# State-space tables on VectorE, merged preparation, value normalisation on ScalarE and modulation dots spread anew in a two-layer hybrid backbone

## Chip, cores and metric

One core of one Trainium2 chip. The metric is the device time of one execution in microseconds, of which the median of several runs is given; lower is better. All inputs are float32 in device memory, and one launch computes the whole output. PE is TensorE, DVE VectorE, ACT ScalarE, POOL GpSimd, SP SyncE (the engine that issues all DMA transfers here, from one queue in order).

## The reference

Two layers run over 256 latent tokens and 256 context tokens of 1024 channels. Layer 0 has a half SwiGLU (width 2816), a mixer and another half SwiGLU; layer 1 the same with attention as the mixer, and needs only the latent tokens after it. Every sub-layer is

```
h = rms(x) * g_pre * (1 + scale) + shift            # per channel
x = x + weight * gate * rms(sublayer(h)) * g_post
shift, scale, gate = columns of silu(c) @ w_mod + b_mod   # 9 x 1024 a layer, for both c
```

The mixer of layer 0 has two groups of heads side by side:

```
p = h @ w_in                                # 768 u, 768 v, 256 for the state-space part
v: gelu, in 6 groups of 128 channels: (v - mean) * rsqrt(var + eps) * g
ya = gelu(u) * (w_s @ v + b_s)              # w_s 128 x 128 over each chunk of 128 tokens
# 16 groups of 16 inputs, 64 complex states, two directions (the second runs backwards)
lam_bar = exp(lam * dt);  b_bar = (lam_bar - 1) / lam * b
s[t] = lam_bar * s[t-1] + b_bar @ u[t];     yb = real(c @ s) + d * u, then gelu and a gate
```

## The kernel before, in words

Channels or features lie on the 128 partitions. A weight chunk of 1 MB (128 x 2048) is loaded by SP into `wraw` (2 buffers), rounded on ACT to `whi` and subtracted on DVE to `wlo` (3 buffers each; `load_upto`, L662 and L663), two chunks ahead of its use; every product is three matmuls (high by high, low by high, high by low). The order of PE and POOL is that of the program text. DVE, ACT and SP are ordered by a planner with an estimated cost for each instruction; on the chip each engine then works through its list strictly in that order. `issue_after(mark)` keeps an instruction from being placed before another one, here mostly the latest gate product of the SwiGLU (L921).

*The first SwiGLU* (`ffn` with `extra=True`) has 22 weight tiles f; tiles 0 to 2 belong to the opening, and `rest(f)` does one of the others: 48 matmuls of 512 columns. After it come 11 chunks of the out projection (`out_proj`), of which the first 8 run over all four token tiles; the last 3 are held for the end, token by token, each followed by `finish` (gate, residual, norm of the next sub-layer).

*Modulation dots.* A column block of w_mod (128 columns, transposed) is multiplied with silu(c) by one DVE instruction with accumulation for each c (L702), two for most blocks and one for the 32 that only the latent needs. One block is a job: one load into `mraw` (2 buffers) and its dots. 128 jobs are handed out in order: `mods(n)` adds n to what is due and issues as many; `mods_need` issues at once whatever a boundary still lacks: `gate_rows` wants the gate's blocks, `scale_cols` the next sub-layer's shift and scale.

*State-space preparation* (`S5Prep`). `angles` and `phasors` compute cos and sin of the step's angle and square them repeatedly on [128,16] tiles on DVE (`cmul`, `unit`), `small` the decays' powers (copied into LP and WP by `put`). `table` builds powers E of the unit phasor by doubling, 1 to 128 steps in 7 levels, for a direction and half of the 8 pairs of groups: four tables, on POOL, in a single buffer `s5E`. `table_out` stores each to device memory (L227). `pair(q)` multiplies the coefficients with B and C on DVE into zero-padded block matrices `s5bd` and `s5cz`, `pair_pe(q)` transposes and multiplies them on PE (L281, L292), `pair_out` stores the result. `s5_jobs` says after which tile f each is emitted: tables at 4, 6, 8, 10, their stores two tiles later, pairs at 12 to 19 and their PE parts one tile later. So tile f of the text is followed on PE by the transposes of pair f-13.

*The mixer* (`mixer0`): value products `value(b, w, t)` on PE for three chunks b of 256 columns and four token tiles t (24 matmuls each), gelu on ACT, mean and variance on DVE; `norm(b, t)` takes two token tiles at once: variance to DVE's copy, rstd on POOL (L751, L752), then four `tensor_scalar` on DVE (L1129). `mix(b)` is the product with w_s. Between them, `slot(k)` holds `states(k)` (PE products L355; then eight multiplications and additions and four scans on DVE, giving H) and, two slots later, `read_out(k - 2)` (PE, L389, reads H). `fill` copies the inputs u that L355 reads.

Of the kernel before, what the change touches and what calls it, by code (L numbers as in the profile page):

```python
# [40 lines left out]
class S5Prep:  # L41


    def __init__(self, K, pool, dram, small, d_bc):
# [8 lines left out]
        self.n2 = pool.tile([128, 16], I32, name="s5n2")  # L53

# [49 lines left out]
    def cmul(self, ore, oim, are, aim, bre, bim):  # L104
        V = self.K.nc.vector
        m = self.nw
        t, u = self.new(), self.new()
        V.tensor_tensor(t, are, bre, op=ALU.mult)
        V.tensor_tensor(u, aim, bim, op=ALU.mult)
        V.tensor_tensor(t, t, u, op=ALU.subtract)  # L110
        V.tensor_tensor(u, are, bim, op=ALU.mult)
        V.tensor_tensor(oim, aim, bre, op=ALU.mult)
        V.tensor_tensor(oim, oim, u, op=ALU.add)
        V.tensor_copy(ore, t)
        self.nw = m

    def unit(self, re, im):
        V = self.K.nc.vector
        m = self.nw
        t, u = self.new(), self.new()  # L120
        V.tensor_tensor(t, re, re, op=ALU.mult)
        V.tensor_tensor(u, im, im, op=ALU.mult)
        V.tensor_tensor(t, t, u, op=ALU.add)
        V.tensor_scalar(t, t, -0.5, 1.5, op0=ALU.mult, op1=ALU.add)
        V.tensor_tensor(re, re, t, op=ALU.mult)
        self.last = V.tensor_tensor(im, im, t, op=ALU.mult).ins
        self.nw = m

    def angles(self):
# [3 lines left out]
        self.dt, a, s, c = (self.new() for _ in range(4))  # L133
        self.cs = c, s
        self.exp(self.dt, ls)
        V.tensor_tensor(a, lim, self.dt, op=ALU.mult)
        self.sincos(s, c, a)

        self.ph = (self.new(), self.new())
        V.tensor_copy(self.ph[0], c)  # L140
        V.tensor_scalar(self.ph[1], s, -1.0, None, op0=ALU.mult)
        for _ in range(2):
            self.cmul(*self.ph, *self.ph, *self.ph)
            self.unit(*self.ph)

    def phasors(self):

        self.steps = [self.ph]
        for k in range(1, 7):
            br, bi = self.new(), self.new()  # L150
            self.cmul(br, bi, *self.steps[k - 1], *self.steps[k - 1])
            self.unit(br, bi)
            self.steps.append((br, bi))

    def small(self, r4):
# [4 lines left out]
        c, s = self.cs  # L160
# [7 lines left out]
        P = [(self.new(), self.new()) for _ in range(5)]  # L168
        V.memset(P[0][0], 1.0)
        V.memset(P[0][1], 0.0)  # L170
        V.tensor_tensor(P[1][0], er, c, op=ALU.mult)
        V.tensor_tensor(P[1][1], er, s, op=ALU.mult)
        for m in range(2, 5):
            self.cmul(*P[m], *P[m - 1], *P[1])

        def put(dst, src, i):
            for d in range(2):
                V.tensor_copy(dst[:, :, d, i[d]], src[:, d * 8:d * 8 + 8])

        for m in range(5):  # L180
            for ri in range(2):
                put(LP[:, ri], P[m][ri], (m, 4 - m))
        nre, den, wre, wim, t = (self.new() for _ in range(5))
        V.tensor_scalar(nre, P[1][0], -1.0, None, op0=ALU.add)
        V.tensor_tensor(den, lre, lre, op=ALU.mult)
        V.tensor_tensor(t, lim, lim, op=ALU.mult)
        V.tensor_tensor(den, den, t, op=ALU.add)
        V.reciprocal(den, den)
        V.tensor_tensor(wre, nre, lre, op=ALU.mult)
        V.tensor_tensor(t, P[1][1], lim, op=ALU.mult)  # L190
        V.tensor_tensor(wre, wre, t, op=ALU.add)
        V.tensor_tensor(wre, wre, den, op=ALU.mult)
        V.tensor_tensor(wim, P[1][1], lre, op=ALU.mult)
        V.tensor_tensor(t, nre, lim, op=ALU.mult)
        V.tensor_tensor(wim, wim, t, op=ALU.subtract)
        V.tensor_tensor(wim, wim, den, op=ALU.mult)
# [1561 lines left out]
```

## Time and profile before

| | before |
|---|---|
| time, median of 3 runs | 1644.54 us (1643.34 to 1649.43) |
| profiled execution, its own time | 1647.93 us |
| its span | 1646.2 us |
| PE busy | 1591.2 us, 97% |
| DVE busy | 1156.3 us, 70% |
| ACT busy | 645.7 us, 39% |
| POOL busy | 167.5 us, 10% |
| mean PE clock granted | 0.986 of full |

The span runs from the first to the last instruction of the profiled execution; its own time contains a little more around it. Busy shares are averages over stages that have different limits, so the stages have to be read one by one: a wait names the instruction that waited, what released it, the total, how many times and the longest. The matmuls' records overlap, so a busy PE only says that something was in the array. In the profile's names, `out<-in` is the tile written and the tiles read.

### The profile page before, as it was taken

Reading aid. Unit: us, or ns where it says so; the run is one execution under the profiler, and the core shown is the slowest. Engines: PE = TensorE matmul, PEld = TensorE weight load, DVE = VectorE, ACT = ScalarE, POOL = GpSimd, SP = SyncE. Lnnn points to the kernel's source line nnn. Section 1 sums busy time; section 2 is a strip of 40 time slices with the busy share of each in tenths; the row PEclk is TensorE's granted clock in tenths of the full one; section 3 lists DMA queues with packets and bytes.
Section 4 is the critical chain, followed back from the end, with each engine's and each line's share of the span. In section 5 each row is a group of like instructions: output and inputs, shape, how many; then the busy total and the mean of one; then the engine's idle time right before and its main releaser. Section 6 shows DMA issues by size and latency. Waiting matters only on the chain.

```text
span 1646.2 us, 23111 instructions
## 1 busy us (share of the span) xinstructions
PE 1591.2 (97%) x8916; PEld 1377.4 (84%) x8916; DVE 1156.3 (70%) x2242; ACT 645.7 (39%) x1023; POOL 167.5 (10%) x289
## 2 busy tenths in 40 slices
PE   6999779999998999999999999999999999999998
PEld 6888668888897789888888889999988877899986
DVE  6797288777689976888786367688864377576454
ACT  5422122322553454222222254466532266564343
POOL 0178600000010000000000010000000012400000
PEclk7999989999999999999999999999999999999999
DMA  9344456545335432656666222222355232146552
GB/s 366 126 160 146 153 194 194 198 171 203 138 119 180 153 125 107 226 195 218 217 225 251 100 103 77 77 103 103 124 210 179 77 119 103 65 177 248 191 192 102
DMA packets 56542, 264.04 MB, mean 160 GB/s; under 512 B 6432, under 2 KB 10992, under 8 KB 36848
## 3 DMA queue, kind: packets, MB, share of 16 engines
q1 hardware_dynamic: 56432, 262.57, 44.7%
q8 instruction: 70, 1.15, 0.3%
q14 instruction: 40, 0.33, 0.1%
HBM read 254.12 MB, written 8.43 MB: 159 GB/s over the span
## 4 chain that ended last, share of the span: by engine, by line
PE 61%; DVE 4%; issue 1%; ACT 1%; POOL 1%; POOLq 0%; DVEq 0%; ACTq 0%
PE y L823 7%; PE y L826 7%; PE y L824 7%; PE gu L816 3%; PE gu L815 3%; PE gu L817 3%; PE u L817 2%; PE g L817 2%; PE g L816 2%; PE u L816 2%; PE g L815 2%; PE u L815 2%; PE sa L534 2%; PE sa L536 2%; PE sa L535 2%
## 5 line engine op out<-in xcount | busy, mean ns | idle before, releaser
L662 ACT ACTIVATE whi<-wraw 128x2048 fp32r<-128x2048 f32 (+1 forms) x139 | 255.3, 1839 | 324.2 <-PE u L816 129.9
L663 DVE TENSOR_TENSOR wlo<-wraw,whi 128x2048 fp32r<-128x2048 f32 x131 | 300.4, 2294 | 102.1 <-ACT whi L662 101.8
L702 DVE SCALAR_TENSOR_TENSOR junkv<-mraw,cond 128x1024 bf16<-128x1024 f32 x224 | 274.6, 1226 | 89.6 <-DMA mraw<-wmod 87.3
L823 PE MATMUL y<-whi,ahi 128*128 128x512 f32 x616 | 243.7, 396 | 0.0
L824 PE MATMUL y<-wlo,ahi 128*128 128x512 f32 x616 | 243.0, 394 | 0.0
L826 PE MATMUL y<-whi,alo 128*128 128x512 f32 x616 | 198.3, 395 | 0.0
L816 PE MATMUL gu<-hlo,whi 128*128 128x256 f32 x496 | 138.7, 280 | 0.7 <-DVE hlo L807 0.7
L823 PEld LDWEIGHTS y<-whi,ahi 128*128 128x128 f32 x616 | 116.1, 188 | 27.1
L826 PEld LDWEIGHTS y<-whi,alo 128*128 128x128 f32 x616 | 116.0, 188 | 27.1
L815 PE MATMUL gu<-hhi,whi 128*128 128x256 f32 x496 | 138.6, 279 | 0.0
L824 PEld LDWEIGHTS y<-wlo,ahi 128*128 128x128 f32 x616 | 116.1, 188 | 26.8
L817 PE MATMUL gu<-hhi,wlo 128*128 128x256 f32 x496 | 138.3, 279 | 0.0
L746 POOL TENSOR_TENSOR ssy<-ssy,mh 128x1 f32<-128x1 f32 x20 | 11.8, 589 | 1220.9 <-DVE ssy L745 1220.9
L1035 ACT ACTIVATE ahi<-act 128x1024 fp32r<-128x1024 f32 (+1 forms) x44 | 41.6, 951 | 227.8 <-PE y L824 216.0
L817 PE MATMUL g<-hhi,wlo 128*128 128x512 f32 x328 | 129.3, 394 | 0.0
L817 PE MATMUL u<-hhi,wlo 128*128 128x512 f32 x328 | 129.2, 394 | 0.0
L816 PE MATMUL g<-hlo,whi 128*128 128x512 f32 x328 | 128.8, 393 | 0.0
L816 PE MATMUL u<-hlo,whi 128*128 128x512 f32 x328 | 128.6, 392 | 0.0
L815 PE MATMUL g<-hhi,whi 128*128 128x512 f32 x328 | 128.5, 392 | 0.0
L1036 DVE TENSOR_TENSOR alo<-act,ahi 128x1024 fp32r<-128x1024 f32 (+1 forms) x44 | 47.8, 1091 | 113.4 <-ACT ahi L1035 113.4
L815 PE MATMUL u<-hhi,whi 128*128 128x512 f32 x328 | 127.3, 388 | 0.0
L816 PEld LDWEIGHTS gu<-hlo,whi 128*128 128x128 f32 x496 | 93.1, 188 | 1.2 <-DVE hlo L807 1.1
(370 smaller groups left out, 3372.2 us busy)
## 6 DMA issues: line engine op xcount, KB each, us to landing
wraw<-wts SPq DMA_DIRECT2D x153, 1024.0 KB, 4.8
mraw<-wmod SPq DMA_DIRECT2D x131, 512.0 KB, 4.3
gg<-gg SPq DMA_DIRECT2D x10, 512.0 KB, 4.9
s5p<-dP SPq DMA_DIRECT2D x8, 384.0 KB, 4.9
act<-wmod SPq DMA_DIRECT2D x5, 512.0 KB, 8.7
act<-wsc SPq DMA_DIRECT2D x5, 512.0 KB, 8.5
dP<-s5cz SPq DMA_DIRECT2D x8, 320.0 KB, 2.3
dP<-s5st SPq DMA_DIRECT2D x8, 320.0 KB, 4.4
```

The costliest lines, as they stand in the source:

```text
L534: nc.tensor.matmul(o, w1[:, k], b1[:, k], start=(new and k == 0), stop=False, skip_group_check=not new)
L662: nc.scalar.activation(h, r, AF.Copy)
L663: (nc.gpsimd if pool else nc.vector).tensor_tensor(l, r, h.bitcast(F32), op=ALU.subtract)
L702: nc.vector.scalar_tensor_tensor(self.junk_v, t, 1.0, self.cond[:, s], op0=ALU.mult, op1=ALU.mult, accum_out=self.mod[:, layer, s, idx * 8 ...
L815: nc.tensor.matmul(out, w1, self.hhi[:, k, sl], start=(k == 0), stop=False)
L816: nc.tensor.matmul(out, w1, self.hlo[:, k, sl], start=False, stop=False)
L817: nc.tensor.matmul(out, w2, self.hhi[:, k, sl], start=False, stop=(k == 7))
L823: nc.tensor.matmul(o, ahi, whi[i], start=first, stop=False)
L824: nc.tensor.matmul(o, ahi, wlo[i], start=False, stop=False)
L826: nc.tensor.matmul(o, alo, whi[i], start=False, stop=last)
L1035: nc.scalar.activation(hi, src, AF.Copy)
L1036: nc.vector.tensor_tensor(lo, src, hi.bitcast(F32), op=ALU.subtract)
```

## The change

Six edits, all in layer 0 or in the handing out of the dots:

1. `table` runs on DVE; the real and the imaginary part are handled by one instruction (four instead of six a level). Tables with q0 = 0 stay in the buffer that `s5cz` shares, those with q0 = 4 lie in the buffer of the pairs' products (`s5tbc`), and two scratch tiles are shared with `s5st` and `s5bd`.
2. The complex helpers keep real and imaginary part in one [128,2,16] tile: `square` does 8 instructions where `cmul` and `unit` did 13, `cmul` 4 instead of 7; `put` is 18 ACT copies instead of 36 on DVE.
3. Tables are emitted at f = 4, 5, 6, 7, their stores one tile later, `zero` at 8, pairs at 9 to 16, their PE parts at 10 to 17.
4. Value normalisation: one small DVE instruction makes -mean x rstd, and the four big ones become ACT activations (Identity with scale and bias).
5. Dots: nothing in the opening and up to f = 5, then 1.2, 1.9 and 2.6 jobs a tile; 3 instead of 2.5 a chunk in the first out projection; the last two chunks of every out projection's main part give half; none in the mixer. `scale_cols` moves from ahead of the out projection to the first `finish`.
6. The value product of chunk 1, token tile 1, comes ahead of `slot(0)`.

```diff
-    def cmul(self, ore, oim, are, aim, bre, bim):
+    def cmul(self, o, a, b):
...
+        V.tensor_tensor(t, a, self.on2(b[:, 0]), op=ALU.mult)
+        V.tensor_tensor(u, a, self.on2(b[:, 1]), op=ALU.mult)
+        V.tensor_tensor(o[:, 0], t[:, 0], u[:, 1], op=ALU.subtract)
+        V.tensor_tensor(o[:, 1], t[:, 1], u[:, 0], op=ALU.add)
...
+    def square(self, o, a):
...
+        V.tensor_tensor(t, re, im, op=ALU.subtract)
+        V.tensor_tensor(u, re, im, op=ALU.add)
+        V.scalar_tensor_tensor(o[:, 1], re, 2.0, im, op0=ALU.mult, op1=ALU.mult)
+        V.tensor_tensor(o[:, 0], t, u, op=ALU.mult)
+        V.tensor_tensor(z, o, o, op=ALU.mult)
+        V.tensor_tensor(t, z[:, 0], z[:, 1], op=ALU.add)
         V.tensor_scalar(t, t, -0.5, 1.5, op0=ALU.mult, op1=ALU.add)
+        self.last = V.tensor_tensor(o, o, self.on2(t), op=ALU.mult).ins
...
         def put(dst, src, i):
             for d in range(2):
-                V.tensor_copy(dst[:, :, d, i[d]], src[:, d * 8:d * 8 + 8])
+                self.K.nc.scalar.activation(dst[:, :, :, d, i[d]], src[:, :, d * 8:d * 8 + 8], AF.Copy)
...
     def table(self, d, q0, pool):
+        V = self.K.nc.vector
+        if q0 == 0:
+            E = pool.tile([128, 4, 2, 128], F32, name="s5E", tag="s5big", bufs=1)
+        else:
+            E = pool.tile([128, 1152], F32, name="s5tb", tag="s5tbc", bufs=1)[:, 0:1024]
...
         for k in range(7):
             n = 1 << k
...
+            V.tensor_tensor(t, E[:, :, :, 0:n], b_r, op=ALU.mult)
+            V.tensor_tensor(u, E[:, :, :, 0:n], b_i, op=ALU.mult)
+            V.tensor_tensor(E[:, :, 0, n:2 * n], t[:, :, 0], u[:, :, 1], op=ALU.subtract)
+            V.tensor_tensor(E[:, :, 1, n:2 * n], t[:, :, 1], u[:, :, 0], op=ALU.add)
...
                 if c:
-                    self.mods(self.mod_rate)
+                    self.mods(self.mod_rate if c < n0 - 2 else self.mod_rate / 2)
...
         gg = self.gate_rows(layer, j, weight, streams)
-        if nxt:
-            self.scale_cols(*nxt)
+        todo = [nxt] if nxt else []
         def finish(t, y):
+            if todo:
+                self.scale_cols(*todo.pop())
...
-                if not extra or f < NF - 2:
+                if extra:
+                    self.mods(0 if f < 6 else 1.2 if f < 10 else 1.9 if f < 18 else 2.6)
+                else:
                     self.mods(self.mod_rate)
...
-                self.mod_rate = 2.5 if extra else 1.75
+                self.mod_rate = 3 if extra else 1.75
...
-            at(4 + 2 * i, pr.table, d, q0, pool)
-            at(6 + 2 * i, pr.table_out, d, q0)
-        at(11, pr.zero, pool)
+            at(4 + i, pr.table, d, q0, pool)
+            at(5 + i, pr.table_out, d, q0)
+        at(8, pr.zero, pool)
         for q in range(8):
-            at(12 + q, pr.pair, q, pool)
-            at(13 + q, pr.pair_pe, q, pool)
-            at(13 + q, pr.pair_out, q)
+            at(9 + q, pr.pair, q, pool)
+            at(10 + q, pr.pair_pe, q, pool)
+            at(10 + q, pr.pair_out, q)
...
                 self.rstd(r, 4)
+                nb = rs[:, 8 + 2 * t - 2:8 + 2 * t + 2]
+                V.scalar_tensor_tensor(nb.rearrange("p (t g) -> p t g", g=2), mv[:, t - 1:t + 1, :, 0], -1.0,
+                                       r.rearrange("p (t g) -> p t g", g=2), op0=ALU.mult, op1=ALU.mult)
                 for i in (t - 1, t):
                     for g in range(2):
                         v = vh[:, i, g * 128:(g + 1) * 128]
-                        V.tensor_scalar(v, v, mv[:, i, g, 0:1], rs[:, 2 * i + g:2 * i + g + 1],
-                                        op0=ALU.subtract, op1=ALU.mult)
+                        k = 2 * i + g
+                        nc.scalar.activation(v, v, AF.Identity, scale=rs[:, k:k + 1], bias=rs[:, 8 + k:9 + k])
...
-                if g >= 4:
-                    self.mods(2)
...
+            value(1, w2, 1)
             for h in hu.values():
                 self.let(h)
             slot(0)
...
-        with self.tc.issue_after(prep.last):
-            self.mods(3 * self.mod_rate)
```

## Rows read from the trace of the kernel before

**Rows 1.** The page, busy time, share of the span and instructions of each engine.

```profile
PE 1591.2 (97%) x8916; PEld 1377.4 (84%) x8916; DVE 1156.3 (70%) x2242; ACT 645.7 (39%) x1023; POOL 167.5 (10%) x289
```

**Rows 2.** Waits of PE, whole span: total us, times, longest us.

```profile
PE wbt L281 <- DVE s5bd L267: 18.1, 1, 18.1
PE s5yp L389 <- DVE s5H L376: 6.2, 3, 3.0
PE s5x L355 <- ACT u L339: 2.0, 1, 2.0
```

**Rows 3.** Windows: stretch and length, busy time (instructions) by engine, PE clock, DMA share, GB/s.

```profile
98.50:142.40 43.90, 43.90 (x194) 36.01 (x193) 42.95 (x153) 9.81 (x8) 34.66 (x46) 1.00 0.48 163
164.30:197.40 33.10, 33.10 (x145) 26.86 (x143) 8.67 (x13) 4.80 (x4) 26.17 (x58) 1.00 0.30 113
197.40:215.50 18.10, 0.03 (x1) 0.00 (x0) 10.69 (x29) 4.31 (x3) 0.95 (x1) 0.65 0.73 253
215.50:220.00 4.50, 4.46 (x24) 3.45 (x25) 4.47 (x10) 1.67 (x5) 0.00 (x0) 0.53 0.40 114
225.00:300.00 75.00, 75.00 (x406) 61.13 (x405) 60.64 (x191) 23.54 (x42) 0.00 (x0) 1.00 0.58 186
476.20:528.00 51.80, 45.53 (x321) 42.73 (x320) 47.27 (x134) 18.70 (x39) 6.92 (x10) 0.96 0.40 130
```

**Rows 4.** Waits of the DMA queue on SyncE, 40 to 300 us.

```profile
SPq L227 <- POOL s5E L224: 60.4, 3, 23.2
```

**Rows 5.** Timeline of SyncE's queue: start, duration, instruction (fourth store of a table).

```profile
196.35 0.38 SPq L227 DMA_DIRECT2D dE<-s5E  x1
```

**Rows 6.** Timeline of DVE, with the idle time before the instruction.

```profile
204.79 1.23 DVE L702 SCALAR_TENSOR_TENSOR junkv<-mraw,cond 128x1024 bf16<-128x1024 f32 x1 [17.46 <-DMA mraw<-wmod]
```

**Rows 7.** Timeline of DVE at the POOL row of the next group.

```profile
134.64 2.28 DVE L663 TENSOR_TENSOR wlo<-wraw,whi 128x2048 fp32r<-128x2048 f32 x1
```

**Rows 8.** Timeline of POOL, table instructions of several sizes.

```profile
134.70 2.54 POOL L224 TENSOR_TENSOR s5E<-s5Et 128x128 f32<-128x128 f32 x1
167.09 0.46 POOL L224 TENSOR_TENSOR s5E<-s5Et 128x128 f32<-128x128 f32 x1
175.31 0.10 POOL L210 MEMSET s5E<- 128x4 f32 x1 [3.59 <-DMA dE<-s5E]
```

**Rows 9.** Groups on DVE, 476.2 to 528 us: count, busy, mean ns, idle before.

```profile
L374 DVE TENSOR_TENSOR s5Q<-s5G,s5e 128x508 f32<-128x508 f32 x10 | 6.5, 681 | 0.1
L377 DVE TENSOR_TENSOR s5H<-s5Q 128x254 f32<-128x254 f32 x5 | 2.1, 419 | 0.0
L1129 DVE TENSOR_SCALAR vh<-vh,mv,rsv 128x128 f32<-128x128 f32 x20 | 5.7, 343 | 4.1 <-POOL rsv L752 4.1
```

**Rows 10.** Group on DVE by form, 52 to 135 us, the preparation's products.

```profile
L113 DVE TENSOR_TENSOR s5w<-s5w 128x16 f32<-128x16 f32 x14 | 3.0, 212 | 0.1
```

**Rows 11.** Timeline of ACT in the mixer's opening.

```profile
454.83 0.39 ACT L1115 ACTIVATE vh<-v 128x256 f32<-128x256 f32 x1 [1.10 <-PE v L1114]
455.45 1.02 ACT L803 ACTIVATE h<-tp,mod,A 128x256 f32<-128x256 f32 x2 [0.23 <-PE tp L794]
```

**Rows 12.** Groups on DVE, 225 to 300 us: dots, weight subtractions, gate products.

```profile
L702 DVE SCALAR_TENSOR_TENSOR junkv<-mraw,cond 128x1024 bf16<-128x1024 f32 x14 | 17.0, 1217 | 0.0
L663 DVE TENSOR_TENSOR wlo<-wraw,whi 128x2048 fp32r<-128x2048 f32 x6 | 13.8, 2293 | 0.2
L921 DVE TENSOR_TENSOR act<-u,act 128x512 f32<-128x512 f32 x6 | 4.2, 692 | 14.1 <-PE wbt L281 14.1
```

**Rows 13.** Timeline of DVE, most of one pair, first and last row of it.

```profile
222.18 0.69 DVE L249 TENSOR_TENSOR s5tb<-s5wp,s5bc 128x128 f32<-128x128 f32 x3
225.98 0.26 DVE L269 SCALAR_TENSOR_TENSOR s5cz<-s5tc 64x80 f32<-64x80 f32 x1
```

**Rows 14.** Timeline of PE, read-outs that waited.

```profile
504.88 0.82 PE L389 MATMUL s5yp<-s5H,s5p 128*128 128x128 f32 x4 [2.71 <-DVE s5H L376]
527.09 1.22 PE L389 MATMUL s5yp<-s5H,s5p 128*128 128x128 f32 x4 [2.95 <-DVE s5H L376]
```

More of the change, by code (lines that the diff above doesn't have):

```diff
@@ L167, in small @@
         LP = pool.tile([128, 2, 8, 2, 5], F32, name="s5lp")
[L168 to L172, printed above, removed]
+        P = [self.new2() for _ in range(5)]
+        V.memset(P[0][:, 0], 1.0)
+        V.memset(P[0][:, 1], 0.0)
+        V.tensor_tensor(P[1], self.cs, self.on2(er), op=ALU.mult)
         for m in range(2, 5):
-            self.cmul(*P[m], *P[m - 1], *P[1])
+            self.cmul(P[m], P[m - 1], P[1])
@@ L196, in small @@
-        V.tensor_tensor(wim, wim, den, op=ALU.mult)
+            put(LP, P[m], (m, 4 - m))
+        den, t, n, z = self.new(), self.new2(), self.new2(), self.new2()
+        V.tensor_scalar(n[:, 0], P[1][:, 0], -1.0, None, op0=ALU.add)
+        V.tensor_copy(n[:, 1], P[1][:, 1])
+        V.tensor_tensor(t, lam, lam, op=ALU.mult)
+        V.tensor_tensor(den, t[:, 0], t[:, 1], op=ALU.add)
+        V.reciprocal(den, den)
+        V.tensor_tensor(t, n, self.on2(lre), op=ALU.mult)
+        V.tensor_tensor(z, n, self.on2(lim), op=ALU.mult)
@@ L198, in small @@
+        W = [self.new2() for _ in range(4)]
+        w = W[0]
+        V.tensor_tensor(w[:, 0], t[:, 0], z[:, 1], op=ALU.add)
+        V.tensor_tensor(w[:, 1], t[:, 1], z[:, 0], op=ALU.subtract)
+        V.tensor_tensor(w, w, self.on2(den), op=ALU.mult)
         WP = pool.tile([128, 2, 8, 2, 4], F32, name="s5wp")
@@ L200, in small @@
             if m:
-                self.cmul(wre, wim, wre, wim, *P[1])
-            for ri, w in ((0, wre), (1, wim)):
-                put(WP[:, ri], w, (3 - m, m))
+                self.cmul(W[m], W[m - 1], P[1])
+            put(WP, W[m], (3 - m, m))
         self.LP, self.WP = LP, WP
     def table(self, d, q0, pool):
-        G = self.K.nc.gpsimd
-        E = self.E = pool.tile([128, 4, 2, 128], F32, name="s5E", tag="s5big", bufs=1)
-        G.memset(E[:, :, 0, 0:1], 1.0)
-        G.memset(E[:, :, 1, 0:1], 0.0)
@@ L213, in table @@
+        i0 = d * 8 + q0
         for k in range(7):
             n = 1 << k
[L215 to L221 removed]
@@ L222, in table @@
-            G.tensor_tensor(t, er, b_i, op=ALU.mult)
-            G.tensor_tensor(u, ei, b_r, op=ALU.mult)
-            G.tensor_tensor(E[:, :, 1, n:2 * n], t, u, op=ALU.add)
+            b_r, b_i = (z[:, i0:i0 + 4].unsqueeze(2).unsqueeze(3).to_broadcast([128, 4, 2, n]) for z in (self.steps[k][:, r] for r in range(2)))
+            t, u = (z[:, 0:8 * n].rearrange("p (q r s) -> p q r s", q=4, r=2) for z in tmp)
+            V.tensor_tensor(t, E[:, :, :, 0:n], b_r, op=ALU.mult)
+            V.tensor_tensor(u, E[:, :, :, 0:n], b_i, op=ALU.mult)
@@ L244, in pair @@
         B = [self.bc[:, q, :, k, :] for k in range(4)]
-        tb = pool.tile([128, 4, 2, 4, 16], F32, name="s5tb")
-        tc_ = pool.tile([128, 4, 2, 5, 16], F32, name="s5tc")
+        both = pool.tile([128, 1152], F32, name="s5tb", tag="s5tbc", bufs=1)
+        tb = both[:, 0:512].rearrange("p (k d j c) -> p k d j c", k=4, d=2, j=4)
+        tc_ = both[:, 512:1152].rearrange("p (k d j c) -> p k d j c", k=4, d=2, j=5)
         def prod(out, coef, mat, n):
@@ L276, in pair_pe @@
         bd, cz = self.bd, self.cz
-        st = pool.tile([128, 640], F32, name="s5st")
+        st = pool.tile([128, 640], F32, name="s5st", tag="s5st", bufs=1)
         ps = K.ps("wbt")
@@ L1105, in value @@
                                mp.tile([128, NT, 2, 2], F32, name="mv", bufs=2),
-                               mp.tile([128, 8], F32, name="rsv", bufs=2))
+                               mp.tile([128, 16], F32, name="rsv", bufs=2))
                 vh, mv, rs = vals[b]
@@ L1186, in mixer0 @@
                     for t in (2 * h, 2 * h + 1):
-                        if (b, t) != (1, 0):
+                        if (b, t) not in ((1, 0), (1, 1)):
                             value(b, w, t)
```

78 lines of the change are left out of this document (27 added, 51 removed).

## The prediction

> **What bounds the kernel now.** The page's busy line comes first: TensorE (PE) works 1591 of 1646 us [rows 1], so only some 55 us can come back without taking matmuls away, and the change takes none away. The waits of PE say where those us are [rows 2]: one wait of 18.1 us of the preparation's first transposes (L281) for block matrices that VectorE (DVE) builds, three of 6.2 us in all in the mixer (L389, for the states H), and one of 2.0 us there (L355). What else PE waits for lies in the start, in the attention and at the end, which the change leaves alone.
>
> The windows around the 18.1 us [rows 3] show that DVE is not slow there but starved: 42.95 busy of 43.9 us from 98.5 on, 8.67 of 33.1 from 164.3 on. The DMA queue says why [rows 4, 5]: SyncE's in-order queue waited 60.4 us, in three waits, for the tables s5E that GpSimd (POOL) computes, since each table's store stands in the queue ahead of weight and modulation loads; the fourth store, the last to wait, went out at 196.35. The first dot behind it ran at 204.79 after 17.46 us of idle DVE [rows 6], the wanted blocks only after 211. In the stretch that follows the clock is 0.53 of full [rows 3]. So the chain is: POOL's fourth table, SyncE, loads, DVE, PE.
>
> POOL is slow because it runs beside DVE: one table instruction, 128x128 elements, took 2.54 us at 134.70, when DVE had begun a 128x2048 subtraction 0.06 us earlier [rows 7, 8], and 0.46 us at 167.09 [rows 8], in the stretch where DVE mostly idles.
>
> **The change part by part.**
>
> *Tables on DVE.* A table is 2 memsets and 7 levels of 4 instructions, 28 in all, over 4 x (1+2+...+64) x (2+2+1+1) = 3048 elements. The nearest DVE rows are 0.681 us for 508 and 0.419 for 254 [rows 9]: 1.03 ns an element and 0.157 us fixed. So a table is 28 x 0.157 + 3.1 = 7.5 us, four are 30 us; with independent instructions overlapping perhaps 24. The upper bound for one is the whole of POOL's last table, 175.31 to 196.35, 21 us, if DVE were as slow [rows 5, 8]. I take 7.5, as the rows are DVE's own with both inputs in SBUF.
>
> *Merged preparation.* Eight squarings go from 13 to 8 instructions (-40), six complex products from 7 to 4 (-18), 36 copies go to ScalarE (ACT) as 18, four others go: 98 fewer on DVE, each up to 0.21 us [rows 10], about half overlapped: 10 to 20 us less. ACT gets 18 small copies, at most 0.51 us each by a larger one [rows 11], 9 us where ACT is busy 9.81 of 43.9 [rows 3]. I cost them at nothing; if one waits long in ACT's queue, the weight conversion behind it is late, and it has about one 11 us weight tile of lead.
>
> *Dots moved.* A job is one load and two dots of 1.22 us [rows 12]. Before, the opening gave 3 jobs and weight tiles f=3 to f=9 eight more; now f=6 to 9 give 4, f=10 to 17 fifteen (was ten) and f=18 to 21 eleven (was two). The out projection gives 18 instead of 17. So 48 jobs are done before the mixer, which needs just 48: its 7 jobs, 17 us of DVE, go, though they lay after 553 us, where PE never waited, so I give that nothing. By the same count 3 jobs (one dot each) are now forced in the second mixer, none before: 0 to 3 x 1.22 = 3.7 us. Their loads and dots have no predecessor there and can be placed long before; I take 0.
>
> *Is DVE still in time?* The first transposes now stand after f=10 instead of f=13, at 164.3. From 98.5 to there are 65.8 us. DVE owes: tables 30, dots of four jobs 9.8, six weight subtractions of 2.29 [rows 12] 13.8, six gate products of 0.69 [rows 12] 4.1, what is left of the preparation about 6 (estimate), the first pair 4.1 [rows 13]: 67.8. That is 2 over, but the dots are wanted by nobody until the boundary, and the tables, emitted at f=4 to 7, can run in the stretch from 143 on where DVE now lies idle. Bounds: 0 to 4 us of PE wait; I take 0. Then the pairs follow, one a tile: now 75 us hold six tiles with theirs (six subtractions, [rows 12]) and DVE is busy 60.64 of them [rows 3], 10.1 of 12.5 a tile; 0.7 more jobs a tile add 1.7, so 11.8: covered, with little to spare.
>
> Here a rule speaks against the change. The Trainium skill, "Perfetto Trace Analysis", section "Optimizing Scalar/DVE Operations", says to offload a saturated DVE to ScalarE or even GpSimd; the tables go the other way, onto a DVE that is 98% busy from 98.5 to 142.4. By it DVE would fall behind, and the time is the slower rival's. The same section warns that the two share an SBUF port, so that work on GpSimd may not help; the 2.54 against 0.46 us above agree with that. By it DVE gets back waits that its 42.95 contain, and the 67.8 falls under 65.8. The sum holds the second, the rival the first.
>
> So the store of a table waits for an engine whose pace the planner foresees better, the loads behind it go on, and the 18.1 us go. The slow stretch goes too: 4.5 us at 0.53 are 2.4 at full clock, 2.1 saved. Late next would be the first pair's blocks, by the 0 to 4 above. First stage: 20.2.
>
> *Mixer.* From 476.2 to 528 DVE is busy 47.27 of 51.8, and idle 4.1 of the rest for POOL's rstd [rows 3, 9]; PE waits there for H 2.71 and 2.95 [rows 14], and the clock over the whole stretch is 0.96 [rows 3], so up to 0.04 x 51.8 = 2.1 are lost to it. The value normalisation leaves DVE: 20 instructions at a pitch of 0.26 (four in 1.03 to 1.12 us) are 5.2, and five small ones of about 0.12 come: 4.6 gained, plus up to 4.1 if those no longer stand where DVE idles. ACT takes them: 24 at up to 0.51 is 12 us, with 18.70 busy of 51.8, and the mix that reads them comes a value chunk later. The two kinds of activation already follow each other there with 0.23 us between [rows 11]. What waits behind an ACT instruction held by rstd is the next weight conversion, 1 to 2 us.
>
> The value product put ahead of the first states (24 matmuls at 0.118, 2.8 us) covers the 2.0 of L355, but PE then only comes 2 us earlier to the first read-out, which already waits for H. It pays what DVE's chain gives, about 0.5. Bounds of the mixer: PE's waits 6.2 + 2.0 and the 2.1 of clock, 10.3 at most; none, or 2 us worse, if the planner puts a weight subtraction before H again. I take 5, DVE's relief.
>
> *Sum.* The profiled execution took 1647.9 around a span of 1646.2, 3.4 above the median of 1644.5. 1647.9 - 18.1 - 2.1 - 5 = 1622.7; from the median, 1619.3. I say 1620.
>
> **Rivals.**
> A. Both happen (forecast): 1613 to 1628. For it: rows 4 to 8, a chain with one cause.
> B. The stall shrinks but stays: a store waits in SyncE for a table queued behind dots on DVE, or DVE's debt comes due at the first transposes. Half the 20 us is lost: 1619 + 10 = 1629, and 1634 without the mixer's 5. For it: the 67.8 against 65.8. Against: the stores may slip to f=8 with a tile in hand.
> C. The change doesn't do what it says, as the wait was the loads' and not the tables': when SyncE was free, 7.4 us passed to the first dot and 10.7 to the blocks. Then 18.1 remains elsewhere and only the mixer pays: 1640. Against it: nothing else held SyncE so long.
> D. Slower: DVE runs out in f=4 to 10. If a table cost 21 us on it, four are 84 instead of 30, the debt is 67.8 + 54 - 65.8 = 56 and PE waits that long for weights and blocks: 1620 + 56 = 1676. It decides from a table of 7.5 + 25/4 + 8/4 = about 16 us, where the whole gain and 8 us more are eaten. Against it: the rows give 7.5, and DVE waits for POOL's port less.
>
> **How the numbers follow.** A 0.66, B 0.21, C 0.06, D 0.07. Within 0.5% (8.2 us, about what a measurement here can tell) is 1636.3 to 1652.8: C, and a little of B's upper end, less what of B stays faster, 0.08; slower is D, 0.07; faster 0.85. The low end, 1610, is the mixer's whole 10.3 and 4 for unknowns; the high end, 1640, takes in B and C and leaves out D and single us. A alone would be 1613 to 1628.
>
> **What would show it.** Right: no wait of L281 over 4 us and PE's clock at 1.00 from 100 to 400 us; SyncE's wait for s5E under 20 us in all and named DVE; no POOL instruction of s5E; a table in 7 to 9 us of DVE; L389 waiting under 3 us in all, L355 none. Wrong: L281 waiting at most of its eight places or weight subtractions late (B, D), or L389's waits still 6 us, when the mixer's bound was not those normalisations. If the mixer loses its waits and the time still stays above 1635, the first stage is where I erred.

## The result and the profile after

| | before | after |
|---|---|---|
| time, median of 4 runs each, side by side | 1645.56 us (1643.34 to 1649.43) | 1629.08 us (1627.02 to 1631.25) |
| ratio after to before | | 0.9888, 95% interval 0.9871 to 0.9906 |
| profiled execution | 1647.93 us | 1627.31 us |
| its span | 1646.2 us | 1625.5 us |

The change made the kernel 1.1% faster, about 16.5 us by the medians and 20.6 us between the two profiled executions. The forecast was 1620. The steps below are compared between the profiled executions, as the sum of the prediction was.

The busy line of the page, to be held against [rows 1]: PE does the same matmuls, POOL has lost 97 us of work, DVE has gained 6.5 in all.

```profile
PE 1586.1 (98%) x8916; PEld 1374.8 (85%) x8916; DVE 1162.8 (72%) x2246; ACT 657.4 (40%) x1065; POOL 70.3 (4%) x113
```

The waits of PE over the whole span (total us, times, longest us). Line numbers have moved: L289 is the former L281, L363 the former L355, L394 and L397 the two parts of the former L389 (products with u and with H), L802 the transposes of the next sub-layer's norm.

```profile
PE s5yp L394 <- DVE u L349: 4.1, 1, 4.1
PE s5yp L397 <- DVE s5H L384: 4.1, 1, 4.1
PE tp L802 <- DVE xn L788: 2.9, 2, 2.7
```

No wait of the preparation's transposes is left, and none of L363, where [rows 2] had 18.1 and 2.0 us. But the waits of the mixer, three for H (6.2 us) and the 2.0 of the states' products, have become two at one place that come to 8.2 us, as much as before, and there is a new one of 2.7 us.

The same windows as the first, second and fifth of [rows 3] (stretch and length, busy time and instructions by engine, clock, DMA share, GB/s):

```profile
98.50:142.40 43.90, 43.90 (x193) 36.06 (x192) 39.52 (x133) 10.07 (x9) 0.00 (x0) 1.00 0.44 156
164.30:197.40 33.10, 33.10 (x185) 26.99 (x183) 31.91 (x95) 11.57 (x21) 0.00 (x0) 1.00 0.67 226
225.00:300.00 75.00, 75.00 (x368) 61.29 (x367) 61.40 (x123) 23.77 (x31) 0.00 (x0) 1.00 0.59 204
```

DVE has taken nearly all of the four tables into the first of them (the last one ends at 144.7) and is nevertheless less busy there than before, 39.5 us against 42.95. In the second it works 31.9 us where it lay idle for a load. SyncE's queue still waits with the tables' stores, 23.1 us where [rows 4] had 60.4, but never over 6.5 at a time:

```profile
SPq L234 <- DVE s5tb L231: 11.7, 2, 6.5
SPq L234 <- DVE s5E L231: 11.4, 2, 6.1
```

How far the 20.2 us came through is read from when PE starts the mixer's first value product and when it starts the state-space gate's product at the mixer's end (`glu`); the rows give the first and last start of a group. Before:

```profile
L1112 PE MATMUL v<-whi,hhi x96: 276/281/366, 449.0 to 501.4; 128*128 128x256 f32 x96
...
L1215 PE MATMUL glu<-s5y,glw x8: 592/592/592, 558.7 to 561.7; 128*128 128x512 f32 x8
```

After:

```profile
L1123 PE MATMUL v<-whi,hhi x96: 275/277/370, 431.6 to 490.7; 128*128 128x256 f32 x96
...
L1228 PE MATMUL glu<-s5y,glw x8: 592/593/593, 538.0 to 541.0; 128*128 128x512 f32 x8
```

The first value product after starts at 431.6 us, 17.4 us earlier. The first `glu` comes 20.7 earlier, so the mixer, from the one to the other, went from 109.7 to 106.4 us. From there on the lead stays: the second layer's first products start at 1046.8 and 1026.1.

**The 2.7 us that are missing ahead of the mixer.** PE stands in the tail of the first out projection, after the first transpose of the next norm (start, duration, instruction, idle time before it):

```profile
412.90 0.27 PE L802 MATMUL tp<-ident,xn 128*128 128x128 f32 x1
415.88 1.86 PE L802 MATMUL tp<-ident,xn 128*128 128x128 f32 x15 [2.71 <-DVE xn L788]
```

and DVE's list at that time has, behind seven dots since 396 us, a weight subtraction ahead of the norm's xn:

```profile
412.25 2.29 DVE L671 TENSOR_TENSOR wlo<-wraw,whi 128x2048 fp32r<-128x2048 f32 x1 [0.27 <-ACT whi L670]
...
415.34 0.88 DVE L788 TENSOR_SCALAR xn<-x,ssx 128x512 f32<-128x512 f32 x2 [0.73 <-POOL ssx L754]
```

**The mixer's opening.** On PE, the products of states 0 and 1 now run without a wait, and the first read-out stands still for 8.2 us of 8.6:

```profile
456.80 1.95 PE L363 MATMUL s5x<-u,s5w 128*128 128x128 f32 x16
...
468.47 0.46 PE L394 MATMUL s5yp<-u,s5p 128*128 128x128 f32 x2 [4.08 <-DVE u L349]
473.00 1.20 PE L397 MATMUL s5yp<-s5H,s5p 128*128 128x128 f32 x4 [4.07 <-DVE s5H L384]
```

DVE shows why. The states' first multiplication (L373) begins at 464.58, 7.8 us after PE began the products it reads. Between them DVE has, in this order, statistics of chunk 0's token tiles 2 and 3, the new small instruction of their normalisation (L1138), which waits 1.49 us for POOL's rstd, a weight subtraction, and copies of u. Of the value product put ahead only two statistics (L1129) stand there, 0.49 us:

```profile
460.49 0.16 DVE L1138 SCALAR_TENSOR_TENSOR rsv<-mv,rsv 128x4 f32<-128x4 f32 x1 [1.49 <-POOL rsv L760]
460.60 2.29 DVE L671 TENSOR_TENSOR wlo<-wraw,whi 128x2048 fp32r<-128x2048 f32 x1
...
463.42 0.49 DVE L1129 BATCH_NORM_STATS2 bst<-vh 128x6 f32<-128x128 f32 x2
...
464.58 0.66 DVE L373 TENSOR_TENSOR s5P<-s5x,s5e 128x512 f32<-128x512 f32 x1
...
472.30 0.16 DVE L1138 SCALAR_TENSOR_TENSOR rsv<-mv,rsv 128x4 f32<-128x4 f32 x1 [1.24 <-POOL rsv L760]
...
472.47 0.39 DVE L384 TENSOR_TENSOR s5H<-s5Q 128x254 f32<-128x254 f32 x1
```

That the first L1138 is not the moved product's is told by ACT, which makes that product's gelu only after it:

```profile
461.27 0.38 ACT L1126 ACTIVATE vh<-v 128x256 f32<-128x256 f32 x1
```

The second L1138 is the one of chunk 1's tiles 0 and 1, the moved product among them; its wait of 1.24 us stands right ahead of H (L384). After this place PE waits for nothing more in the mixer's state-space products; the 2.71 and 2.95 of [rows 14] are gone.

**The mixer's length.** Its waits come to 8.2 us before and after, and yet it is 3.3 us shorter. The windows from the first value product to the first `glu`, before and after, and the one of the stall:

```profile
449.00:558.70 109.70, 101.22 (x692) 93.47 (x691) 96.31 (x257) 46.73 (x105) 9.41 (x16) 0.97 0.41 143
431.60:538.00 106.40, 97.93 (x691) 90.88 (x690) 89.16 (x236) 56.27 (x129) 10.19 (x16) 0.97 0.42 143
468.00:476.00 8.00, 3.46 (x16) 3.33 (x17) 6.70 (x22) 4.14 (x8) 2.41 (x2) 0.57 0.12 35
```

PE was busy 101.2 us before and 97.9 after, with the same products. Before, its clock fell twice, at the two late waits of [rows 14], and products ran at the lower clock (0.79 from 504 to 512 and from 525 to 533). After, it fell once, and mostly while PE stood in the stall: 0.57 from 468 to 476, with PE busy 3.46 of 8 us. The mean clock is 0.97 in both.

### The profile page after: what moved, and what is told of

Same layout as the page of the kernel before. It is cut to its first block, busy times and chain, and to the rows that moved or that the text cites. A ratio compares the mean times of both kernels' runs of the same rounds, so it can differ in the third digit from the quotient of the medians.

```text
span 1625.5 us, 22970 instructions
## 1 busy us (share of the span) xinstructions
PE 1586.1 (98%) x8916; PEld 1374.8 (85%) x8916; DVE 1162.8 (72%) x2246; ACT 657.4 (40%) x1065; POOL 70.3 (4%) x113
## 4 chain that ended last, share of the span: by engine, by line
PE 63%; DVE 4%; issue 1%; ACT 1%; POOL 1%; POOLq 0%; DVEq 0%; ACTq 0%
PE y L831 7%; PE y L834 7%; PE y L832 7%; PE gu L824 3%; PE gu L823 3%; PE gu L825 3%; PE u L825 3%; PE g L825 3%; PE u L824 2%; PE g L824 2%; PE g L823 2%; PE u L823 2%; PE sa L542 2%; PE sa L544 2%; PE sa L543 2%
## 5 line engine op out<-in xcount | busy, mean ns | idle before, releaser
L823 PEld LDWEIGHTS gu<-hhi,whi 128*128 128x128 f32 x496 | 93.3, 188 | 0.1
```

The costliest lines, as they stand in the source:

```text
L823: nc.tensor.matmul(out, w1, self.hhi[:, k, sl], start=(k == 0), stop=False)
```

## The experiments

Twelve kernels ran, four at a time beside the kernel before: E1 to E4, E5 to E8, E9 to E12. Before's median was 1647.60, 1646.86 and 1648.28 us in the three groups, so runs of different groups are compared by their ratio to it. The table has them all; "mixer from" is the start of the first value product, "mixer" the time from it to the first `glu`, and "waits" the part of it that PE waited at its state-space products (s5x and s5yp), from each profile.

| run | what it is | median us | ratio to before, 95% interval | mixer from | mixer | waits |
|---|---|---|---|---|---|---|
| E1 | state-space edits alone | 1630.29 | 0.9886 (0.9871 to 0.9901) | 429.3 | 111.1 | 8.5 |
| E2 | dots spread anew alone | 1636.35 | 0.9931 (0.9919 to 0.9943) | 440.4 | 110.9 | 7.0 |
| E9 | E1 with the tables on POOL | 1637.41 | 0.9933 (0.9918 to 0.9948) | 438.4 | 109.9 | 7.9 |
| E8 | the change with the tables on POOL | 1627.73 | 0.9882 (0.9868 to 0.9897) | 433.9 | 106.6 | 8.5 |
| E10 | E1 with the old tiles | 1627.73 | 0.9881 (0.9864 to 0.9898) | 428.1 | 109.8 | 8.6 |
| E5 | the change again | 1629.70 | 0.9897 (0.9879 to 0.9915) | 432.4 | 108.2 | 8.2 |
| E3 | the change, normalisation on DVE | 1631.46 | 0.9905 (0.9891 to 0.9919) | 431.8 | 110.2 | 10.7 |
| E4 | the change, no value product ahead | 1624.20 | 0.9853 (0.9836 to 0.9871) | 430.1 | 103.3 | 5.5 |
| E11 | E4 again | 1624.15 | 0.9857 (0.9839 to 0.9874) | 432.3 | 103.2 | 5.6 |
| E7 | the change without both mixer edits | 1629.45 | 0.9891 (0.9876 to 0.9906) | 429.6 | 108.3 | 8.6 |
| E6 | E4 with 2.5 jobs a chunk | 1625.93 | 0.9870 (0.9855 to 0.9885) | 428.5 | 105.9 | 4.2 |
| E12 | state-space edits and normalisation on ACT | 1624.95 | 0.9858 (0.9838 to 0.9878) | 432.0 | 105.0 | 5.4 |

The opening alone moves a profile by up to 5 us: in the runs with the new tiles and no stall before it, the first transpose of L289 starts between 162.2 and 167.1. So small differences in "mixer from" are read against that row of the same run, not between runs. A mixer's length holds its waits and what a lower clock costs: less its waits it is 97.6 and 97.8 us in E11 and E4, whose clock is 1.00 throughout, and 98.1 to 103.9 in all others, the change included. Two profiles of the same kernel (the change and E5, 106.4 and 108.2) differ by 1.8 with the same waits. So the waits tell an edit's effect better than the length.

### What removed the first stall

**E1, the state-space edits alone** (edits 1 to 3).

> The kernel before with the state-space edits alone: tables on VectorE, merged real and imaginary parts, ACT copies, tables and pairs emitted 1 to 4 tiles earlier. Dots, value normalisation and the mixer's order stay as before. Theory (tables on POOL beside a full DVE were slow, held their buffer, their stores and with these the weight loads): the transposes of L289 wait under 4 us in all, the first value product of the mixer starts at 429 to 433 us (449 before), the mixer keeps its old waits (s5x 2.0, s5yp 2.7 and 2.9 us), time 1624 to 1629 us, so as fast as the whole change or faster. Rival (the dots that were moved out of the opening and the early tiles made room on DVE and in the queue): the transposes still wait 10 us or more, 1636 us or more.

Measured: no wait of L289, first value product at 429.3, 0.9886; the time of 1630.29 lies a little above the theory's 1624 to 1629. The mixer keeps the waits of before:

```profile
PE s5yp L397 <- DVE s5H L384: 6.4, 3, 2.9
PE s5x L363 <- ACT u L347: 2.1, 1, 2.1
```

The state-space edits are enough for all of the first stage's gain, and the interval is that of the whole change. So edits 4 to 6 together brought nothing that these runs can tell from zero.

**E2, the dots alone** (edit 5).

```diff
-                if not extra or f < NF - 2:
+                if extra:
+                    self.mods(0 if f < 6 else 1.2 if f < 10 else 1.9 if f < 18 else 2.6)
...
-        with self.tc.issue_after(prep.last):
-            self.mods(3 * self.mod_rate)
```

> The kernel before with the spreading of the modulation dots alone; tables stay on POOL at their old tiles. Theory: POOL's tables and their held stores stay, so the transposes of L281 still wait 10 to 20 us, 1638 to 1646 us. Rival (the dots' new places carried the gain of the first stage): the wait falls under 5 us and the time is 1627 to 1632 us. Both: if the dots make the 2.7 us wait of the first out projection's tail (L794 for DVE's xn), it shows here too, at 10 to 20 us before the first value product.

Neither theory nor rival holds. With POOL's tables untouched, the wait went from 18.1 to 5.0 us, PE came to the mixer 8.6 us earlier, and the kernel is 0.7% faster. Waits of PE, then of SyncE's queue:

```profile
PE wbt L281 <- DVE s5bd L267: 5.0, 2, 4.2
```

```profile
SPq L227 <- POOL s5E L224: 36.1, 4, 16.9
```

With the early dots gone POOL's tables came sooner; DVE has 33.1 us of work from 100 to 150 us, 43.0 before. Most of the difference is made by the second table, which took 19.7 us from its memset to its last addition and 36.5 before; the third and fourth, 22.8 and 24.7, were no quicker than before (22.9 and 21.0). POOL cleared the buffer for the fourth at 153.98, in [rows 8] at 175.31:

```profile
153.98 0.10 POOL L210 MEMSET s5E<- 128x4 f32 x1 [3.67 <-DMA dE<-s5E]
```

So the dots in the early tiles were a part of the cause that the prediction had priced at nothing. The 2.7 us in the out projection's tail, which both were to show, did not come: DVE makes the norm's xn at 421.84 there and the weight subtraction behind it, at 424.01.

**E9, E1 with the tables on POOL.**

```diff
     def table(self, d, q0, pool):
-        V = self.K.nc.vector
+        V = self.K.nc.gpsimd
```

> The state-space edits alone, as in the run with the state-space edits, but the tables on POOL: new form, new tiles, two buffers; the dots stay where they were before, two of them in the opening's tiles and the first five. What this leaves open after the last run (POOL's tables were fast enough with the dots gone from the early tiles). Theory (dots beside POOL's tables stretch them and stand behind the held stores in SP's queue): the transposes of L289 wait 5 to 20 us, 1634 to 1645 us. Rival (the new form and the second buffer are enough on either engine): under 2 us, 1628 to 1632 us.

The time and the size came as the theory has them, the place did not: PE waits at a weight tile, not at the transposes. This profile shows the whole chain at once. PE:

```profile
149.56 0.79 PE L825 MATMUL g<-hhi,wlo 128*128 128x512 f32 x1 [6.36 <-DVE wlo L671]
```

DVE: the dot ahead of that weight subtraction had waited 12.11 us for its load.

```profile
145.08 1.70 DVE L710 SCALAR_TENSOR_TENSOR junkv<-mraw,cond 128x1024 bf16<-128x1024 f32 x1 [12.11 <-DMA mraw<-wmod]
...
146.71 2.80 DVE L671 TENSOR_TENSOR wlo<-wraw,whi 128x2048 fp32r<-128x2048 f32 x1
```

SyncE: that load was issued right behind the third table's store, which had waited 14.2 us for POOL.

```profile
135.81 0.38 SPq L234 DMA_DIRECT2D dE<-s5E  x1
136.27 0.46 SPq L661 DMA_DIRECT2D wraw<-wts  x1
136.82 1.41 SPq L708 DMA_DIRECT2D mraw<-wmod  x2
```

Two lists that run in order, SyncE's and DVE's, hand the wait on: table, store, load of w_mod, dot, weight, PE. The first transposes start 9.6 us later than in E1 (174.0 against 164.4): the 6.4 of this wait, and a clock of 0.84 from 149 to 170 us behind it.

Held against the kernel before, E9 is also a gain: its ratio of 0.9933 is 11 us, E1's 0.9886 19. So with the tables still on POOL more than half of E1's gain is there, from the merged form, the second buffer, the smaller preparation and the earlier tiles together; the engine brings the rest. Those four were not taken apart, but for the tiles with the tables on DVE (E10).

**E8, the whole change with the tables on POOL.** The same edit on the changed kernel, whose dots have left the early tiles.

> The changed kernel with the four tables on POOL in place of DVE, in their new merged form and at their new early tiles, in the two buffers of the change. Theory (it is the engine: POOL's instructions take 0.4 to 2.7 us beside a busy DVE, so four tables last some 100 us, and the stores and the pairs' buffer wait for them): the transposes of L289 wait 10 to 40 us, 1638 to 1665 us. Rival 1 (it is the early place and the second buffer, or the dots moved out of the way; POOL is fast enough): they wait under 5 us, 1624 to 1632 us, within 2 us of the whole change. Rival 2 (POOL's time frees DVE): faster than the whole change by 2 us or more.

The theory is wrong and rival 1 right: no wait of L289, and a ratio equal to the change's (0.9882 against 0.9888 and 0.9897). The queue waits for POOL no less than in E9, 43.6 us against 50.0:

```profile
SPq L234 <- POOL s5tb L220: 18.2, 2, 12.3
SPq L234 <- POOL s5tb L231: 17.1, 1, 17.1
SPq L234 <- POOL s5E L220: 8.3, 1, 8.3
```

But the dots' loads come only after the last of these stores, at 144.33; DVE waited for one of them, 6.2 us, and PE not at all. E1, E8, E9 and the change are the four combinations of engine and dots in the new form (E8 and the change hold the mixer's edits too, which lie behind this stage): only POOL with early dots is slow. In the new form either cut is enough: a table that is soon ready, or no dot that must wait behind its store. In the old form, with one buffer, the dots' move alone left 5.0 us (E2).

**E10, E1 with the old tiles** (tables at 4, 6, 8, 10, pairs from 12).

> The state-space edits without the earlier tiles: tables on DVE in their new form, emitted after tiles 4, 6, 8 and 10, pairs after 12 to 19, dots as before. Theory (the earlier tiles are no part of the gain; a table of DVE is done in 7 to 10 us and holds nothing): the transposes wait under 4 us, 1628 to 1632 us. Rival (the earlier tiles carry it): they wait 8 us or more, 1636 us or more.

As the theory has it: no wait of the transposes, 0.9881. Emitting the work earlier is no part of the gain.

### What the mixer's edits do

**E5, the whole change again**, as a partner for the others.

> The whole change again, as the partner of the three others of this call. 1627 to 1632 us; 106 to 107 us from the first value product to the first glu product, with the stall of about 8 us at the first read-out.

The ratio is 0.9897, and the stall at the first read-out is the same (4.08 and 4.05 us). The mixer took 108.2 us, not 106 to 107: the clock stayed low longer behind the stall, 0.53 from 476 to 480 us where the first profile has 1.00.

**E3, normalisation back on VectorE.**

```diff
-                        k = 2 * i + g
-                        nc.scalar.activation(v, v, AF.Identity, scale=rs[:, k:k + 1], bias=rs[:, 8 + k:9 + k])
+                        V.tensor_scalar(v, v, mv[:, i, g, 0:1], rs[:, 2 * i + g:2 * i + g + 1],
+                                        op0=ALU.subtract, op1=ALU.mult)
```

> The changed kernel with the value normalisation back on VectorE (four tensor_scalar a pair, as before). Theory (the small STT that waits for POOL's rstd stands in DVE's list where the big ones stood, so the move freed little): first stage as in the changed kernel, the first read-out still waits 6 to 10 us, one or both of the later read-outs wait 1 to 3 us again; 1628 to 1633 us. Rival 1 (normalisations on ACT delay the u copies and so the first read-out): the wait at the first read-out halves, 1623 to 1627 us. Rival 2 (the prediction's: DVE's relief is worth 5 us): 1633 to 1636 us.

The theory's numbers hold (1631.46, the first read-out waits 7.2 us in all, later ones 3.4). That the move freed little does not: the waits are 10.7 us against 8.2 with ACT, and the mixer is 2.0 to 3.8 us longer (110.2 against 108.2 and 106.4). By the times E3 is not told apart from the change; the intervals overlap.

```profile
PE s5yp L397 <- DVE s5H L384: 7.6, 3, 4.2
PE s5yp L394 <- DVE u L349: 3.1, 1, 3.1
```

**E4, no value product ahead; E11, the same again.**

```diff
             for t in (2, 3):
                 value(0, w1, t)
-            value(1, w2, 1)
...
-                        if (b, t) not in ((1, 0), (1, 1)):
+                        if (b, t) != (1, 0):
```

> The changed kernel with the value product of chunk 1, token tile 1 back behind the first states. Theory (the product ahead moves the first states' DVE work behind a statistics pair, the small STT that waits for POOL and a weight subtraction in DVE's list): DVE starts the first states 2 to 4 us earlier against the product that feeds them, the s5x products wait about 2 us again, the first read-out waits 3 to 6 us in place of 8.2; 1625 to 1629 us. Rival (the product ahead fills the wait of the s5x products and costs nothing elsewhere): s5x waits 2 us, the first read-out waits as long as with it, 1630 to 1633 us.

> The changed kernel without the value product ahead, again, beside the others: 1622 to 1627 us, 3 to 6 us under the whole change by the ratio to before (0.985 to 0.988).

Faster than the whole change: 0.9853 and 0.9857, with intervals that end at 0.9871 and 0.9874, where the change's begin at 0.9871 and 0.9879: they hardly overlap. The waits are 5.5 and 5.6 us against 8.2. PE in E4, with the wait of L363 back, and the first read-out waiting 0.5 us in place of 8.2, less than the theory's 3 to 6:

```profile
454.40 1.13 PE L363 MATMUL s5x<-u,s5w 128*128 128x128 f32 x8 [1.94 <-DVE u L349]
...
465.57 0.73 PE L397 MATMUL s5yp<-s5H,s5p 128*128 128x128 f32 x4 [0.53 <-DVE s5H L384]
```

DVE begins the states 2.7 us after their products begin, not 7.8: no weight subtraction stands ahead of them, and the small instruction that waits for rstd now stands behind the scans, when rstd is long there:

```profile
457.14 0.69 DVE L373 TENSOR_TENSOR s5P<-s5x,s5e 128x512 f32<-128x512 f32 x1
...
464.87 0.15 DVE L1138 SCALAR_TENSOR_TENSOR rsv<-mv,rsv 128x4 f32<-128x4 f32 x1
```

The clock is 1.00 through the whole mixer in both runs.

**E7, without both mixer edits.**

> The changed kernel without both mixer edits: normalisation on VectorE and the value product behind the first states; the mixer still has no dots. From the first value product to the first glu product the runs so far took 109.7 us before, 111.1 with the state-space edits alone, 110.2 without the normalisation on ACT, 103.3 without the product ahead, 106.4 with the whole change. Theory (the two edits add: ACT saves 3.8, the product ahead costs 3.1): 107 us, time 1626 to 1629 us. Rival 1 (the dots taken out of the mixer carry the gain, the normalisation on ACT none by itself): 103 to 104 us, 1622 to 1626 us. Rival 2 (only the normalisation carries it): 109 to 111 us, 1629 to 1632 us.

108.3 us and 1629.45: between the theory and rival 2. With E3, E4 and the change it fills the table of two edits. In waits, the normalisation on ACT takes away 3.1 us without the product ahead (8.6 to 5.5) and 2.5 with it (10.7 to 8.2); the product ahead adds 2.1 with the normalisation on DVE (8.6 to 10.7) and 2.7 with it on ACT (5.5 to 8.2). In length the same steps are 5.0, 2.0 to 3.8, 1.9, and 3.1 to 4.9, with the clock's part in them. Rival 1 fails in the waits too: without dots the mixer waits 8.6 us, with them 7.9 to 8.6 (E1, E9, E10).

**E6, 2.5 in place of 3 jobs a chunk, on E4.**

```diff
-                self.mod_rate = 3 if extra else 1.75
+                self.mod_rate = 2.5 if extra else 1.75
```

> The changed kernel with the value product behind the first states again, and with 2.5 in place of 3 dots jobs a chunk of the first out projection, the number of before. Theory (with 3 jobs a chunk more dots are still unread when the out projection's tail begins, and a weight subtraction then stands ahead of the norm's xn in DVE's list): the 2.7 us wait of L802 for DVE's xn falls under 1 us and nothing comes in its place; 1620 to 1624 us. Rival (the boundary wants these blocks at once anyway, so the dots stay where they are): the wait stays, 1623 to 1627 us.

The 2.7 us wait is gone; another of 1.2 us came one token tile later. From the first transpose of L289 to the first value product it is 264.6 us (163.9 to 428.5), in the change, E3, E4, E5, E7, E8 and E11 267.4 or 267.5, in E1, E9 and E12, with the dots of before, 264.4 to 264.9. So in the changed kernel the 2.7 us go with the dots' new rate. The rate alone does not make them, as E2 has it too and no such wait: what counts is whether DVE's list has the weight subtraction ahead of xn. The time did not follow (0.9870): the mixer took 2.6 us more than E4's, at waits that are no longer (4.2 and the 1.2) but with the clock down twice (below). E6 is not told apart from E4.

**E12, the state-space edits and the normalisation alone.**

> The state-space edits and the normalisation on ACT alone: dots where they were before, also in the mixer, no product ahead. Theory (with the tables off POOL the dots' new places are worth nothing on balance: they make the 2.7 us wait at the out projection's tail and take about as much out of the mixer; the normalisation saves 4 to 5 us of the mixer): no wait of L802 at the tail, 106 to 107 us from first value product to first glu product (111.1 without the normalisation), 1624 to 1628 us. Rival (with eight dots still in the mixer DVE stays full and the normalisation frees nothing): 110 us or more, 1629 to 1632 us.

As the theory has it: 0.9858, no wait of L802 in the tail; the mixer, at 105.0, is a little shorter than its 106 to 107. Its waits are 5.4 us, as in E4 and 3.1 under E1's. It equals E4 without touching the dots. These two are the fastest versions found, both 1.4 to 1.5% faster than before, and by the ratios 5 to 7 us faster than the change; E12's interval still overlaps the change's.

```profile
PE s5yp L397 <- DVE s5H L384: 3.5, 4, 2.0
PE s5x L363 <- ACT u L347: 1.9, 1, 1.9
```

## Why the prediction was right, and where it was not

*First stage, 20.2 us.* Right in size: the mixer's first product came 17.4 earlier, and 2.7 of the rest were lost at another place. The terms held: a table cost DVE 7.5 us (four made 30.0 us of busy time, each 9 to 11 from its memset to its last addition), and DVE, which was to owe 67.8 us in 65.8, made PE wait for nothing. Rivals B and D did not come. C did not either, though E8 bears out a part of it: slow tables alone did not hold PE up, only with loads and dots behind their stores (E9). The Trainium skill says that offloading a saturated DVE, even to GpSimd, may make sense ("Perfetto Trace Analysis", section "Optimizing Scalar/DVE Operations"), by which D would have come. This was not borne out with early dots: there the kernel with its tables on DVE is some 7 us faster than with them on POOL (E1 against E9). The Trainium skill's warning of the shared port, in the same section, is in line with POOL's 2.50 and 0.46 us for one size (128x128) in E8.

*The chain that was read from it* was right link by link, but one link was called harmless. "Dots moved" was priced at 0. E2 shows that this edit alone takes 13.1 of the 18.1 us away, and E8 that with it POOL is quick enough in the new form. In [rows 6] the idle DVE instruction was a dot: the row names the link that E2 cut. The prediction cut the chain at the table and took the other cut for nothing; as both were in the change, the sum did not suffer. Nor was the table's end only a matter of the engine: with the tables on POOL, the other state-space edits are worth more than half of E1's gain (E9). "POOL is slow because it runs beside DVE" holds for the second table, 36.5 us against 19.7 with fewer dots, and not for the fourth, which took 21.0 where DVE mostly idled.

*"Dots moved ... I give that nothing"* also missed a cost: in the changed kernel the higher rate in the out projection leaves dots in its tail and a weight subtraction ahead of the norm, 2.7 us (E6). The prediction had counted the jobs per stage, but not what stands in DVE's list where a stage ends.

*Mixer, 5 us.* The normalisation's move took 3.1 us of waits away wherever no product was put ahead (E7 to E4, E1 to E12), 5.0 and 6.1 us of length with the clock: DVE's relief was sized about right. What failed is the step that the value product put ahead "pays what DVE's chain gives, about 0.5": it costs 2.1 to 2.7 us of waits, 1.9 to 4.9 of length. The prediction counted what it does on PE and took from the row of L389 that the first read-out already waits for H, but not what happens on DVE: the states' products come later on PE, and the wait for rstd and a weight subtraction, which without it stand behind, move in front of the states; the moved product's own normalisation then stands in front of H. It had named that price ("none, or 2 us worse, if the planner puts a weight subtraction before H again") and chosen against it. So the two edits cancelled in the waits, 8.2 us before and after, and the 3.3 us that the mixer gained are PE's shorter busy time: the clock fell once, in one long wait, and not twice at shorter ones. That 3.3 lies near 5 is luck. The dots that left the mixer show no effect in the waits (8.6 without them, 7.9 to 8.6 with them); the prediction's nothing for them stands.

*The sum.* Between the profiles 25.2 were forecast and 20.6 measured; 2.7 (tail) and 1.7 (mixer) of the difference of 4.6 are accounted for. The medians differ by 16.5 because before's profiled execution lay 2.4 above its median and after's 1.8 below; the forecast of 1620 was put near the sum made from the median. So the time fell 1 us outside the range given for A alone and well inside the whole one.

*What would show it.* L281 without a wait, clock at 1.00 from 100 to 400 us, no table on POOL and a table in 7 to 9 us of DVE came out so. SyncE's wait for tables, 23.1 us against "under 20", was harmless. L389 "under 3 us in all" failed with 8.2, at the place named above.

*Open.* How much of the two mixer waits is due to the copies of u, to the weight subtraction and to rstd was not taken apart; nor were the state-space edits with the tables on POOL. Why the clock fell behind some waits of 2 us and not behind others (below) wasn't tried.

## What to carry to other kernels

When the wait runs through two in-order lists, name every link, and price each edit at the link that it cuts: two edits that each cut the same chain do not add, and the one priced at nothing may be the cheaper one. A product that is moved ahead to fill a wait on one engine can change the order on another; look there for what now stands in front of the critical chain, above all for a small instruction that waits for a third engine. Split a stage's length into waits and the rest before an edit is given credit: here an edit's waits came out nearly alike in each pair of runs, while the lengths differed by the clock. When a rate of background work is raised, read the list at the stage's end, where the next stage's first product waits.

## What the runs showed of the hardware

The same wait cost different times. In E4 and in E6 PE stood 1.94 us before L363 in the same place; in E4 the clock stayed at 1.00, in E6 it was at its lower level (1.2 of 2.4 GHz) for most of the time from 456 to 460 us:

```profile
456.00:460.00 4.00, 4.00 (x37) 4.00 (x37) 3.78 (x14) 3.11 (x6) 0.00 (x0) 1.00 0.50 203
```

```profile
456.00:460.00 4.00, 4.00 (x27) 4.00 (x26) 3.79 (x13) 2.76 (x8) 0.00 (x0) 0.67 0.35 139
```

27 matmuls in place of 37 ran in these 4 us (the first row is E4's, the second E6's, each a window's busy times and clock); that is some 1.1 us of the 2.6 by which E6's mixer is longer. It happened again at 504 to 508 us, at 0.70. So a difference of one or two microseconds between two mixers in single profiles is not yet a difference of the kernels.

A lower clock in the opening cost nothing that stands out at the next milestone. From 0 to 50 us it was 0.80 in E5 and E11 and 1.00 in the first profile after, and the first transpose of L289 started at 164.9, 164.8 and 164.2, inside the 162.2 to 167.1 of all such runs.

Where POOL and DVE worked at once, DVE's instructions could take longer too: in the rows of E9 a dot takes 1.70 us and a weight subtraction 2.80, where [rows 12] have 1.22 and 2.29 with POOL at rest. It was not always so: the subtraction of [rows 7] kept its 2.28 beside a POOL instruction of 2.54.
